# Two output terms summed ahead of the matmul, and low parts of weights by a negating copy and an accumulating transfer, in the state-space stage of a decoder kernel

## The chip, the cores and the metric

The kernel runs on one core of a Trainium2 chip. The metric is device microseconds of one execution; the profile gives its own span, from the first to the last instruction, beside it.

## What is computed

The reference is a trunk of two layers for 512 tokens of width 1024, in float32. Layer 0 mixes tokens by gated delta-net and sliding-window heads, layer 1 by an S5 state-space mixer. After the mixer each layer has cross-attention into 256 memory tokens and a SwiGLU feed-forward part; every sub-layer ends in a residual sum and a layer norm. The change lies in the S5 mixer of layer 1:

```python
def s5_mixer(u, a_re, a_im, log_dt, b_re, b_im, c_re, c_im, d_skip, w_o, w_g):
    ...
    bu = jnp.einsum('gph,bsgh->bsgp', b_bar, ug.astype(jnp.complex64))
    _, states = lax.associative_scan(_lin_rec_combine, (a_seq, bu), axis=1)
    y = (jnp.einsum('ghp,bsgp->bsgh', c_re.astype(f32), states.real)
         - jnp.einsum('ghp,bsgp->bsgh', c_im.astype(f32), states.imag))
    y = y.reshape(bsz, s, d) + d_skip.astype(f32) * uf
    hid = jax.nn.gelu(y).astype(u.dtype)
    return (hid @ w_o) * jax.nn.sigmoid(hid @ w_g)
```

## The kernel before

**Matmuls in three parts.** A float32 product is made of float32r products. Each operand is kept as a high part (`hi`, rounded to float32r) and a low part (`lo`, what the rounding left out), and `mm3` issues three matmuls: high by high, high by low, low by high. Weights come from DRAM a piece of 512 KB at a time (`_load`): SyncE issues the transfer into `raw` (2 buffers), ScalarE copies it to `hi` (4 buffers), and VectorE subtracts `hi` from `raw` into `lo` (4 buffers). `weights` calls `_load` with a priority of 200 places ahead of the program (`AHEAD`).

**The order.** No instruction is issued while the program is written down. The class `Order` records each call with its operands, and `issue` then simulates the engines by the costs in `cost` and by a single DMA channel, and gives each engine the first instruction in program order whose operands and buffers are there. What comes out is a fixed queue for each engine. The name of a line in the profile is therefore always the same (L422, in `issue`), and groups are told apart by their tiles: `ps` is a PSUM bank, `big` a tile of 128x2048, `t` a temporary of 128x512 (13 buffers), `tiny` one of 128x64.

**The S5 stage.** `s5` goes through 8 blocks of 4 pairs of groups (128 channels each). For each block it loads two table tiles of 1 MB from the scratch in DRAM (`s5m`), transposes the tokens, makes `br` and `bi` (the input products) with 8 float32 matmuls, turns them back with six VectorE operations into `x` and `y`, scans both along the chunks, and turns them forward again: `r1`, `r2`, `i1`, `i2`, each a product of a scan result and a table, shifted by one chunk, with a small memset on GpSimd for the first column. The output bank `yp` is then summed on TensorE for each of 4 pairs from four products: the taps inside the chunk, `r1` and `r2` with table 4, and `i1 - i2` with table 5. GELU, four transposes and a split into high and low part follow.

**Fill.** Between the blocks `s5` takes steps of other work: after each block one step of `fill`, which is the key projection of the second layer (`mem_k(1)`, 4 column blocks with 2 weight loads each), then the value projection (`mem_v(1)`, 2 halves with 4 loads each); from block 5 on also the first half of the gate (`glu_gate`, 4 loads). The value projection holds its 4 loads until both token tiles are done. Just ahead of the stage stands the layer norm of layer 0's feed-forward part, whose result the first transposes read.

Of the kernel before, what the change touches and what calls it, by code (L numbers as in the profile page):

```python
# [92 lines left out]
class Engine:  # L93
    """Records the calls of an engine instead of issuing them."""
# [10 lines left out]
class Order:  # L105
    """The order in which the recorded instructions are issued: for each engine, the first in program
    order of those whose operands are there, by estimates of what the instructions take."""
# [12 lines left out]
    def either(self, *calls):  # L120
        """The same result by one of several engines: (engine, function, args, kwargs)"""
        self.add(list(calls))
# [7 lines left out]
    # ---- what an access touches  # L130
# [40 lines left out]
    @staticmethod  # L171
    def operands(fn, args, kw):
        isap = lambda x: hasattr(x, "ap") and hasattr(x, "tensor")
        conv = lambda x: x if isap(x) else (x[:] if hasattr(x, "mls") else None)
        outs, ins = [], []
        for n, x in [("out" if k == 0 else "", x) for k, x in enumerate(args)] + list(kw.items()):
            x = conv(x)
            if x is None:
                continue
            (outs if n in ("out", "accum_out") else ins).append(x)  # L180
        if fn == "tensor_tensor_reduce":
            outs.append(ins.pop())
        if fn == "matmul" and not kw["start"]:
            ins.append(outs[0])
        return outs, ins

    def cost(self, eng, fn, outs, ins, kw):
        o = outs[0]
        n = 1
        for _, c in list(o.ap)[1:]:  # L190
            n *= c
        psum = any("PSUM" in str(x.space) for x in ins)
        if eng == "pe":
            if fn == "transpose":
                return 0.11
            r = ins[0].dtype == F32R
            if r:
                return (n if n >= 256 else max(4 * n, 128)) / 2400.0 + 0.0035
            m = list(ins[0].ap)[-1][1]
            return (4 * n if n >= m else 2 * (n + m)) / 2400.0 + 0.004  # L200
        if eng == "act":
            ptr = sum(1 for k in ("bias", "scale") if hasattr(kw.get(k), "tensor")) + ("accum_out" in kw)
            return n / 1200.0 + (0.05 if psum else 0.095) + 0.093 * ptr
        if eng == "dve":
            fast = fn in ("tensor_copy", "tensor_scalar", "memset") and not psum and "PSUM" not in str(o.space)
            if fn == "reciprocal":
                return 0.0063 * n + 0.07
            if fn in ("tensor_reduce", "bn_stats"):
                n = max(n, max(_size(x) for x in ins))
            ptr = 0.06 if any(_size(x) == 1 for x in ins) else 0.0  # L210
            return (n / 1.92 if fast else n / 0.96) / 1000.0 + 0.07 + ptr
        if eng == "pool":
            if kw.get("op") == OP.pow:
                return 0.165 * n + 0.3
            return n * 0.00085 + 0.03 if fn == "memset" else n * 0.0022 + 0.1
        return 0.45

    # ---- recording
# [50 lines left out]
    # ---- ordering  # L269
    def order(self, seq, prio):  # L270
# [44 lines left out]
        while len(out) < n:  # L315
# [5 lines left out]
            for e in self.eng:  # L321
# [53 lines left out]
                if e == "sp":  # L375
                    busy[e] = now + a[4]
                    nbytes = max(_bytes(x) for x in op.outs + op.ins)
                    s = max(now + 1.65, dma_free)
                    dma_free = s + nbytes / 3.6e5
                    op.done = dma_free + 0.75  # L380
                else:
                    cost = a[4]
                    if e == "pe":
                        if now - busy[e] > 3.4:
                            slow = now + 3.4
                        cost += min(cost, max(slow - now, 0.0) * 0.5)
                    busy[e] = now + cost
                    op.done = busy[e]
# [55 lines left out]
class Trunk:  # L444
    def __init__(self, tc, a, stack, dbg=None):
        self.tc, self.nc, self.a, self.dbg = tc, tc.nc, a, dbg or {}
        self.o = Order(tc)
        self.n = 0
        self.stack = stack
        pool = lambda name, bufs, **k: stack.enter_context(tc.tile_pool(name=name, bufs=bufs, **k))  # L450
        self.cp = pool("const", 1)
        self.bigp = pool("big", 16)
        self.wp = pool("w", 2)
        self.tp = pool("t", 2)
        self.ps = pool("ps", 8, space=bass.MemoryType.PSUM)
        self.dram = pool("dram", 1, space=bass.MemoryType.DRAM)
# [20 lines left out]
    def weights(self, w, k0, n, c0, width):  # L477
        """n row tiles of w by `width` columns as high and low parts, fetched ahead of the program"""
# [8 lines left out]
    def _load(self, view, n, w, steps=1, between=None):  # L487
# [4 lines left out]
        for s in range(steps):  # L492
# [5 lines left out]
            self.o.V.tensor_tensor(lo[:, cs], raw[:, cs], hi[:, cs].bitcast(F32), op=OP.subtract)  # L498
# [8 lines left out]
    def gemm_feat(self, w, c0, cols, act, n, sink, early=0):  # L507
        """out[feature, token], 256 columns of w at a time; act(kt) -> (hi, lo) of [128, n]. The first
        `early` column blocks take the first half of the tokens before the second."""
# [39 lines left out]
    def gemm_tok_steps(self, w, k0, nk, c0, act, ntt, sink, tail=0):  # L549
        """out[token, 512 columns of w at c0]; act(kt, tt) -> (hi, lo) of [128, 128]. The last `tail`  # L550
        steps of the contraction go one token tile after the other."""
# [20 lines left out]
    def transposes(self, src, n, width=P):  # L572
        """n blocks of [128, width] from src to one bank [width, n, 128]"""
# [9 lines left out]
    def mixer0(self, fill):  # L583
# [6 lines left out]
        # ---- x, transposed  # L590
# [14 lines left out]
        # ---- constants  # L605
# [19 lines left out]
        # ---- rotary tables  # L625
# [14 lines left out]
        # ---- beta and decay logits, feature-major then token-major  # L640
# [57 lines left out]
        # ---- delta-net q, k, v  # L698
# [44 lines left out]
        # ---- the decay inside a chunk, [j, (head, i)]  # L743
# [24 lines left out]
        # ---- chunk matrices, [j, (head, i)]: L^T above its diagonal  # L768
# [25 lines left out]
        # ---- q and v  # L794
# [3 lines left out]
        # ---- inverse of the 32 x 32 diagonal blocks, one system a partition (h, c, b)  # L798
# [17 lines left out]
        # ---- the products of q and k under the decay  # L816
# [12 lines left out]
        # ---- the gate of the delta-net heads  # L829
# [8 lines left out]
        # ---- merge the blocks: X' = X - X E X for 32, 64  # L838
# [41 lines left out]
        # ---- sequential part over chunks  # L880
# [80 lines left out]
        # ---- the sliding-window heads  # L961
# [57 lines left out]
    def feat_view(self, bigs):  # L1019
        """tiles of 2 feature tiles each -> at(kt) of [128, (hi, lo), 512], act(kt), act(kt, tt)"""  # L1020
# [9 lines left out]
    def residual_sinks(self, half, alpha, eps, g, b, last, after):  # L1030
        """z = alpha h + sublayer in place of h; on the last half the norm, then after(tt, h)"""
# [41 lines left out]
    def to_feat(self, vs):  # L1073
        """after-norm step: the token tile transposed into the feature-major operand"""
        return lambda tt, n, x: self.block_to_feat(vs, n, slice(tt * P, (tt + 1) * P), x)
# [147 lines left out]
    # ---- S5  # L1223
    def s5_params(self):
        """per state (g2, p) on partitions and pair of groups q: the discretised coefficients"""
# [20 lines left out]
        # exp(lam) - 1 = 2 t / (1 - t), t = tanh(lam / 2)  # L1246
# [27 lines left out]
        # (a_bar - 1) / a, with a_bar - 1 = (e - 1) - 2 e sin^2(theta / 2) + i e sin(theta)  # L1274
# [17 lines left out]
    def s5_tables(self):  # L1292
        """the matrices of a chunk of 4 tokens for each pair of groups, left in DRAM by blocks of 4 pairs"""
# [5 lines left out]
        # rotations by 0..15 chunks, and by 0, 16, .., 112  # L1299
# [57 lines left out]
        # B [(g2, p), q, h] and C [(g2, p), q, h]  # L1357
# [5 lines left out]
        # the skip on the diagonal of the first tap  # L1363
# [3 lines left out]
        for b in range(8):  # L1367
# [11 lines left out]
            # rotation tables  # L1379
# [12 lines left out]
            # chunk input and output matrices  # L1392
# [28 lines left out]
            # decay over a chunk, none into the first  # L1421
# [4 lines left out]
            # taps inside a chunk  # L1426
# [26 lines left out]
    def s5(self, fill):  # L1453
        """the mixer's output in feature-major form; with it the gate of the first half of the columns"""
# [3 lines left out]
        for b in range(8):  # L1458
# [15 lines left out]
            # turned back by the rotation of each chunk: x - i y  # L1474
# [12 lines left out]
            # forward again, one chunk later; the real part's products meet in the output's sum  # L1487
# [6 lines left out]
            r1, r2, i1, i2 = turned(x, cs), turned(y, sn), turned(x, sn), turned(y, cs)  # L1494
            V.tensor_tensor(i1, i1, i2, op=OP.subtract)
            terms = ((r1, 4), (r2, 4), (i1, 5))
            yp = self.bank()
            for q in range(4):
# [3 lines left out]
                for n, (z, m) in enumerate(terms):  # L1502
                    T.matmul(yo, q1(z, q), kc(m), start=False, stop=n == 2)
# [49 lines left out]
    def exp(self, out, x, w):  # L1553
        """exp to float32: 2^n by the exponent's bits, a polynomial on what is left"""
# [14 lines left out]
    def reduced(self, ang, tmp):  # L1569
        """an angle of any size less a multiple of 2 pi, in parts"""  # L1570
# [18 lines left out]
    def build(self):  # L1589
# [13 lines left out]
        for _ in range(PRE):  # L1603
            next(kv)
        gtok = self.s5(kv)
        self.glu(gtok)
# [28 lines left out]
def layouts(v):  # L1635
    """the inputs as the kernel reads them: small operands with the index that goes on partitions first"""
# [31 lines left out]
```

## Time and profile before

| | us |
|---|---|
| runs | 1576.44, 1580.3, 1572.28 |
| median of the runs | 1576.44 |
| span of the profiled execution | 1572.0 |
| TensorE busy / VectorE busy / ScalarE busy / GpSimd busy | 1539.2 / 990.3 / 550.9 / 58.2 |

The profile gives one execution; its time beside the span is not listed by itself, the nearest of the runs is 1572.28. Busy times are sums over the span. TensorE's records overlap and their ends are modelled, so its busy time is not a measure of the rate at which it works; the distance from one start to the next is.

### The profile page before, as it was taken

How to read it: one execution, taken by the hardware profiler on the slowest of the kernel's cores; microseconds unless marked ns; L12 is line 12 of the kernel's file. 1: busy time of each engine (PE TensorE's matmuls, PEld its weight loads, DVE VectorE, ACT ScalarE, POOL GpSimd, SP SyncE). 2: the span in 40 equal slices, each digit the busy share in tenths (PEclk: the TensorE clock that was granted, in tenths of full speed). 3: DMA queues.
4: the chain of work that ended last, by engine and by line, in shares of the span. 5: the costliest groups of instructions: out<-in, count | busy, mean ns of one | idle time of the engine just before them, and what ended most of it. 6: DMA issues, size and time to landing. Idle time of an engine off the chain costs nothing.

```text
span 1572.0 us, 20938 instructions
## 1 busy us (share of the span) xinstructions
PE 1539.2 (98%) x8132; PEld 1300.8 (83%) x8132; DVE 990.3 (63%) x1890; ACT 550.9 (35%) x988; POOL 58.2 (4%) x97
## 2 busy tenths in 40 slices
PE   7999999999999999999999899999999999999998
PEld 5887878778988888888888798888888888888886
DVE  6989666556557788725754899748657443334436
ACT  6533436424432344423441233332422322222211
POOL 1100000000000000010000000000000000000000
PEclk9999999999999999999999999999999999999999
DMA  6423224125314344526572554323213333233322
GB/s 184 125 60 95 81 89 134 51 71 168 91 37 132 111 166 163 183 84 201 188 254 81 201 176 148 125 94 108 88 37 98 107 102 100 73 115 96 105 68 94
DMA packets 125539, 184.06 MB, mean 117 GB/s; under 512 B 14144, under 2 KB 84800, under 8 KB 121344
## 3 DMA queue, kind: packets, MB, share of 16 engines
q1 hardware_dynamic: 125440, 182.73, 36.0%
q8 instruction: 64, 1.05, 0.3%
q14 instruction: 35, 0.29, 0.1%
HBM read 162.52 MB, written 20.19 MB: 116 GB/s over the span
## 4 chain that ended last, share of the span: by engine, by line
PE 83%; DVE 10%; DMA 2%; ACT 2%; issue 1%; SPq 0%; POOL 0%; DVEq 0%; ACTq 0%; POOLq 0%
PE ps L422 83%; DVE t L422 5%; DVE big L422 3%; DVE lo L422 2%; ACT big L422 1%; ACT hi L422 1%; DVE tiny L422 1%; DMA raw<-in_xv_w_dram 1%; DMA t<-in_x_t_dram 1%; DMA raw<-in_xo_w_dram 0%; DMA raw<-in_hyb_w_in_dram 0%; ACT L422 0%; DMA raw<-in_hyb_w_out_dram 0%; ACT t L422 0%; DMA prm<-in_dn_a_log_dram 0%
## 5 line engine op out<-in xcount | busy, mean ns | idle before, releaser
L422 PE MATMUL ps<-big,hi 128*128 128x512 f32 (+1 forms) x2368 | 651.4, 361 | 6.4 <-ACT hi L422 4.9
L422 PE MATMUL ps<-hi,big 128*128 128x512 f32 x1728 | 548.1, 395 | 1.1 <-DVE big L422 0.7
L422 PEld LDWEIGHTS ps<-big,hi 128*128 128x128 f32 x2368 | 422.1, 191 | 70.0 <-ACT hi L422 5.3
L422 DVE TENSOR_TENSOR lo<-raw,hi 128x1024 fp32r<-128x1024 f32 (+2 forms) x252 | 303.5, 1205 | 222.8 <-ACT hi L422 220.1
L422 ACT ACTIVATE hi<-raw 128x1024 fp32r<-128x1024 f32 (+2 forms) x252 | 263.5, 1046 | 512.2 <-PE ps L422 356.4
L422 PE MATMUL ps<-big,lo 128*128 128x512 f32 (+1 forms) x1184 | 426.7, 362 | 2.7 <-DVE lo L422 2.6
L422 PEld LDWEIGHTS ps<-hi,big 128*128 128x128 f32 x1728 | 323.2, 188 | 66.5 <-DVE big L422 1.6
L422 PE MATMUL ps<-lo,big 128*128 128x512 f32 x864 | 339.1, 394 | 4.6 <-DVE lo L422 4.5
L422 PEld LDWEIGHTS ps<-big,lo 128*128 128x128 f32 x1184 | 225.5, 191 | 34.8 <-DVE lo L422 3.8
L422 PEld LDWEIGHTS ps<-lo,big 128*128 128x128 f32 x864 | 162.8, 188 | 40.3 <-DVE lo L422 8.0
L422 ACT ACTIVATE big<-ps 128x256 fp32r<-128x256 f32 (+2 forms) x196 | 93.9, 514 | 223.2 <-PE ps L422 214.2
L422 DVE TENSOR_TENSOR big<-ps,big 128x256 fp32r<-128x256 f32 (+1 forms) x160 | 82.2, 545 | 63.0 <-ACT big L422 61.1
L422 ACT ACTIVATE t<-ps 128x512 f32<-128x512 f32 (+4 forms) x129 | 64.5, 510 | 161.9 <-PE ps L422 157.9
L422 DVE SCALAR_TENSOR_TENSOR big<-big,ps 128x512 f32<-128x512 f32 x56 | 38.3, 685 | 95.4 <-PE ps L422 95.4
L422 DVE SCALAR_TENSOR_TENSOR t<-t,ps 128x512 f32<-128x512 f32 x72 | 48.9, 681 | 58.5 <-ACT t L422 53.5
L422 PE MATMUL ps<-big,big 128*128 128x256 f32 (+6 forms) x392 | 72.3, 340 | 0.1
L422 ACT ACTIVATE big<-t 32x128 f32<-32x128 f32 (+1 forms) x140 | 59.9, 443 | 30.6 <-DVE t L422 13.2
L422 PEld LDWEIGHTS ps<-big,t 128*128 128x128 f32 (+2 forms) x496 | 59.4, 186 | 10.8 <-issue 3.6
L422 PE MATMUL ps<-big,t 128*128 128x128 f32 (+3 forms) x496 | 65.5, 276 | 1.8 <-DVE t L422 1.7
L422 DVE SCALAR_TENSOR_TENSOR big<-big,tiny,t 128x512 f32<-128x512 f32 x96 | 66.6, 744 | 0.0
L422 PE MATMUL ps<-ident,t 128*128 128x128 f32 x336 | 60.2, 274 | 3.7 <-ACT t L422 1.9
L422 PEld LDWEIGHTS ps<-big,big 128*128 128x128 f32 (+1 forms) x392 | 54.2, 189 | 8.6 <-issue 1.9
(140 smaller groups left out, 927.7 us busy)
## 6 DMA issues: line engine op xcount, KB each, us to landing
raw<-in_ffn_wg_dram SPq DMA_DIRECT2D x44, 512.0 KB, 3.5
raw<-in_ffn_wu_dram SPq DMA_DIRECT2D x44, 512.0 KB, 3.5
raw<-in_ffn_wd_dram SPq DMA_DIRECT2D x44, 512.0 KB, 3.9
s5m<-big SPq DMA_DIRECT2D x16, 1024.0 KB, 4.4
big<-s5m SPq DMA_DIRECT2D x16, 1024.0 KB, 5.2
raw<-in_hyb_w_in_dram SPq DMA_DIRECT2D x26, 512.0 KB, 3.9
raw<-in_xk_w_dram SPq DMA_DIRECT2D x16, 512.0 KB, 4.9
raw<-in_xv_w_dram SPq DMA_DIRECT2D x16, 512.0 KB, 3.8
```

What stands on the lines that cost most here:

```text
L422: op.inst = getattr(self.eng[e], fn)(*args, **kw)
```

## The change

In `s5`, `r1` and `r2` are added on VectorE, in place, and the sum goes through one product with table 4 in place of two. During `s5` (that is, for the loads recorded there: the keys and values of the second layer and the first half of the gate) `_load` makes the low part in another way: ScalarE writes the negated copy of `raw` to `lo`, rounded as `hi` is, and a transfer issued from GpSimd reads the weights from DRAM once more and adds them to `lo`. The subtraction on VectorE goes. The order's model gets a cost of 1.2 us for a DMA issue on GpSimd, treats it as a DMA of the same channel as SyncE's, and counts an accumulating transfer's destination as an input. Comments and docstrings are dropped throughout, which is left out here.

```diff
@@ operands @@
-        if fn == "matmul" and not kw["start"]:
+        if fn == "matmul" and not kw["start"] or kw.get("accum_op"):
             ins.append(outs[0])
@@ cost @@
         if eng == "pool":
+            if fn == "dma_start":
+                return 1.2
@@ order @@
-                if e == "sp":
+                if a[1] == "dma_start":
                     busy[e] = now + a[4]
                     nbytes = max(_bytes(x) for x in op.outs + op.ins)
                     s = max(now + 1.65, dma_free)
@@ _load @@
             self.o.A.activation(hi[:, cs], raw[:, cs], AF.Copy)
-            self.o.V.tensor_tensor(lo[:, cs], raw[:, cs], hi[:, cs].bitcast(F32), op=OP.subtract)
+            if self.low_by_dma:
+                self.o.A.activation(lo[:, cs], raw[:, cs], AF.Copy, scale=-1.0)
+                self.o.G.dma_start(r(lo)[:, ks], view[:, ks], accum_op=OP.add)
+            else:
+                self.o.V.tensor_tensor(lo[:, cs], raw[:, cs], hi[:, cs].bitcast(F32), op=OP.subtract)
@@ s5 @@
             r1, r2, i1, i2 = turned(x, cs), turned(y, sn), turned(x, sn), turned(y, cs)
+            V.tensor_tensor(r1, r1, r2, op=OP.add)
             V.tensor_tensor(i1, i1, i2, op=OP.subtract)
-            terms = ((r1, 4), (r2, 4), (i1, 5))
+            terms = ((r1, 4), (i1, 5))
...
-                    T.matmul(yo, q1(z, q), kc(m), start=False, stop=n == 2)
+                    T.matmul(yo, q1(z, q), kc(m), start=False, stop=n == 1)
@@ build @@
+        self.low_by_dma = True
         gtok = self.s5(kv)
+        self.low_by_dma = False
```

The lines that the model of a DMA goes on with are the same in both kernels:

```python
                    dma_free = s + nbytes / 3.6e5
                    op.done = dma_free + 0.75
```

## Rows read from the trace of the kernel before

**Rows 1.** The page: its span, and the chain that ended last by engine

```profile
span 1572.0 us, 20938 instructions
...
PE 83%; DVE 10%; DMA 2%; ACT 2%; issue 1%; SPq 0%; POOL 0%; DVEq 0%; ACTq 0%; POOLq 0%
```

**Rows 2.** Busy time by 15 us stretches of 885 to 1005 us

```profile
core 0: us, PE busy (x) PEld busy (x) DVE busy (x) ACT busy (x) POOL busy (x), PEclk, DMA share, GB/s
...
900.00:915.00 15.00, 12.94 (x85) 12.73 (x86) 12.68 (x18) 4.18 (x7) 0.32 (x3) 0.77 0.52 176
...
960.00:975.00 15.00, 14.36 (x90) 12.05 (x89) 15.00 (x22) 4.10 (x7) 0.42 (x4) 1.00 0.13 41
...
sum 120.00, PE 113.48 PEld 103.24 DVE 111.05 ACT 41.20 POOL 4.16; mean PE 14.19 PEld 12.90 DVE 13.88 ACT 5.15 POOL 0.52
```

**Rows 3.** The chain inside 875 to 1010 us: start, us, what

```profile
879.68 1.07 ACT hi L422
...
882.60 1.14 DVE lo L422
...
894.54 4.78 DVE t L422 x8
...
902.75 9.10 PE ps L422 x53
```

**Rows 4.** Busy time by longer and shorter stretches, columns as in rows 2

```profile
870.00:930.00 60.00, 55.21 (x387) 52.06 (x386) 54.04 (x84) 16.46 (x23) 4.42 (x17) 0.94 0.58 211
930.00:1005.00 75.00, 73.27 (x457) 63.84 (x457) 69.93 (x99) 26.86 (x41) 1.70 (x16) 1.00 0.37 122
...
885.00:890.00 5.00, 4.47 (x38) 4.27 (x36) 4.96 (x12) 0.00 (x0) 1.51 (x6) 1.00 1.03 413
```

**Rows 5.** Groups by shape, 885 to 1005 us: count, busy us, mean ns, idle before

```profile
L422 PE MATMUL ps<-big,t 128*128 128x128 f32 x226 | 30.1, 279 | 1.2 <-DVE t L422 1.1
...
L422 PE MATMUL ps<-t,big 128*128 128x128 f32 x128 | 16.4, 275 | 0.0
...
L422 ACT ACTIVATE hi<-raw 128x1024 fp32r<-128x1024 f32 x20 | 21.1, 1058 | 20.7 <-DMA raw<-in_xk_w_dram 10.1 <-PE ps L422 8.5 <-DMA raw<-in_xv_w_dram 1.2
```

**Rows 6.** TensorE in order of time: start, us, operation, idle before

```profile
883.56 0.40 PE L422 MATMUL ps<-big,hi 128*128 128x256 f32 x2
...
890.77 1.97 PE L422 MATMUL ps<-ident,big 128*128 128x128 f32 x16 [1.30 <-DVE big L422]
...
902.75 0.58 PE L422 MATMUL ps<-big,lo 128*128 128x256 f32 x1 [2.06 <-DVE lo L422]
...
951.61 3.06 PE L422 MATMUL ps<-big,t 128*128 128x128 f32 x26
954.43 0.48 PE L422 MATMUL ps<-lo,big 128*128 128x512 f32 x1
```

**Rows 7.** VectorE in order of time, columns as in rows 6

```profile
896.26 0.68 DVE L422 TENSOR_TENSOR t<-t,t 128x512 f32<-128x512 f32 x1
896.86 0.68 DVE L422 TENSOR_TENSOR t<-ps,big 128x512 f32<-128x512 f32 x1
```

**Rows 8.** The page's DMA issues: count, KB each, median us to landing

```profile
raw<-in_xk_w_dram SPq DMA_DIRECT2D x16, 512.0 KB, 4.9
raw<-in_xv_w_dram SPq DMA_DIRECT2D x16, 512.0 KB, 3.8
...
raw<-in_s_glu_wg_dram SPq DMA_DIRECT2D x8, 512.0 KB, 4.7
```

**Rows 9.** Issues into the raw tiles, 862 to 1000 us: ns min/median/max

```profile
L422 SPq DMA_DIRECT2D raw<-in_xk_w_dram x8: 367/368/389, 862.8 to 909.5; - x8
```

**Rows 10.** DMA issues from 870 to 930 us, columns as in rows 8

```profile
big<-s5m SPq DMA_DIRECT2D x8, 1024.0 KB, 8.4
```

**Rows 11.** The transfers of the tables, 800 to 1000 us

```profile
DMA to landing us min/median/max: 5.2/5.2/11.7
```

More of the change, by code (lines that the diff above doesn't have):

```diff
@@ L1604, in build @@
             next(kv)
+        self.low_by_dma = True
         gtok = self.s5(kv)
+        self.low_by_dma = False
         self.glu(gtok)
```

## The prediction

> **What bounds the kernel now.** I read the page first. TensorE holds 83% of the chain that ended last [rows 1], which says little yet: its records overlap, so a TensorE that looks busy can still lose time between matmuls. So I went to the stage that the change touches. The S5 stage runs from about 885 to 1005 us: the state-space blocks, filled up with the second layer's key and value projections and the first half of the gate. In its 15 us stretches [rows 2] the reader is to see that VectorE is as full as TensorE: 111.05 us of 120 against 113.48, and 15 of 15 in the middle, where TensorE has 14.36. The chain inside the stage [rows 3] changes sides: a subtraction that makes a low part (`lo`), runs of VectorE pieces on the temporaries, then a run of 53 matmuls. So neither engine alone sets the stage; each is a few per cent from being the bound. Two more things matter. Around 885 us the DMA engines are full (share 1.03, 413 GB/s) [rows 4]. And TensorE's granted clock, 2.4 GHz elsewhere in the stage, is 0.77 in the mean from 900 to 915 us, so part of that stretch went at 1.2 GHz [rows 2], after TensorE had waited several times.
>
> **Matmuls removed: -7.0 us.** Each of 8 blocks drops one of the four products for each of 4 pairs: 32 matmuls. An f32 matmul of this shape stands in the trace as two records: the 64 products that make `br` and `bi` are 128 records [rows 5]. So 64 records go. What one costs TensorE is the distance between starts, not its 279 ns: 26 of them start at 951.61 and the next instruction at 954.43 [rows 6], 2.82/26 = 0.1085 us. 64 x 0.1085 = 6.9, taken as 7.0. The bound on the other side is busy time over count, 30.1/226 = 0.133 [rows 5], or 8.5. This counts only where TensorE is the bound.
>
> **One add a block on VectorE: nothing.** A 128x512 add of two temporaries holds it 0.60 us (896.26 to 896.86 [rows 7]); 8 x 0.60 = 4.8 us. What hides it is the time freed by the 20 subtractions (of the loads in [rows 8], which are for both layers and both halves: 8 for keys, 8 for values, 4 for the gate), each 1.14 us in the chain [rows 3], 22.8 us; net VectorE loses 18 us of work in a stage where it is full. Without that cover the add would cost the 4.8.
>
> **VectorE freed: -3.1 us.** It can only give back time in which TensorE waits. TensorE idles 120 - 113.48 = 6.5 us in the stage [rows 2]. Of that 1.30 stands before the first transposes, which wait for the layer norm, and 2.06 at 902.75 for a low part [rows 6], whose raw weights had come late: ScalarE waited 10.1 us for the keys' weights [rows 5]. Neither ends with VectorE's load. 6.5 - 1.3 - 2.1 = 3.1. The bounds are 0 (other short waits take their place) and 6.5, which adds what the lower clock costs, 15 x 0.23 = 3.4 us [rows 2]. I leave the clock as it is, since the part on the first low parts puts a gap near the same place.
>
> **Negating copies on ScalarE: nothing.** 20 copies like the one of 1.06 us that makes `hi` [rows 5] are 21 us; ScalarE is busy for 41.20 of 120 us [rows 2], so its gaps hold them. Without that cover a PSUM eviction queued behind one comes up to 1.06 us late.
>
> **Issues on GpSimd: nothing.** The kernel before issues no DMA from GpSimd. The price of an issue there is bounded below by SyncE's 0.37 us [rows 9]; above I take the 1.2 us that the new line in the order's costs sets. 20 x 1.2 = 24 us on an engine with 4.16 us of work in the stage [rows 2]. Queued behind an issue that waits for its copy are the small memsets of the turned tiles, four a block; the new add reads their column, so VectorE can wait for them: 1.2 us in each of 8 blocks, 9.6 us, which the 18 us freed cover.
>
> **The first low parts: +4.8 us.** Today `hi` of the first key weights starts at 879.68 on ScalarE [rows 3], and the 48 matmuls of the first key block fill TensorE from 883.56 until 1.30 us before the transposes at 890.77 [rows 6], 5.9 us in which the layer norm runs and TensorE has nothing else. After: copy done at 880.75, negation at 881.8, issue, landing. The shortest landing of a weight load is 3.8 us [rows 8]; the 1 MB table loads of this very stretch, in which the DMA engines are full, take 8.4 in the median [rows 10] and 11.7 at most [rows 11]. So `lo` comes between 885.6 and 893.5, and up to 0.8 us (1.2 - 0.37) later by the issue. I take 890, since the stretch is full. The third matmul of the group needs it, so all 5.9 us of key matmuls move behind the norm and lengthen a stage that is then TensorE's. Against that, the norm loses the subtraction at 882.60, which stands in its chain [rows 3]: S5 starts 1.1 us earlier. 5.9 - 1.1 = 4.8. Bounds: `lo` at 885.6 lets TensorE wait 1.8 us after its first two matmuls, +0.7; `lo` at 894.3 with the transposes queued behind the waiting matmul adds 3.5, +8.3.
>
> **The later low parts: +6.0 us.** 20 loads go through 4 `lo` buffers: five passes, the first priced above. In each, a new low part can start only when TensorE lets go of a buffer. Today the subtraction follows the copy at once. The order written for the changed kernel allows by its own formulas about 0.95 us for the negating copy and 1.65 + 1.46 + 0.75 us for a DMA with free engines, 4.8 in all, and puts other matmuls there. TensorE's queue is fixed, so what comes later than that stalls it. By the rows: 1.06 + 4.9 (median landing of the key weights [rows 8]) + 0.4 (half of 0.8, the issue) = 6.4, so 1.6 a pass; I take 1.5, 4 passes. Bounds: landing 3.8 gives 4.9, nearly 0 a pass; landing 8.4 with 0.8 for the issue gives 10.3, 5.5 a pass, 22 us.
>
> The Trainium skill, "DMA: Bandwidth & Descriptors", section "Anatomy of one DMA — SWDGE (gpsimd) path", fits a transfer issued from GpSimd by 2.0 us plus its bytes over 436 GB/s; for 512 KB that is an estimate of 3.2 us, shorter than any landing in [rows 8], and by it the later passes would cost nothing and the sum would be 6 us lower. The Trainium skill, "Collectives: The Full Stack", section "The bandwidth ceiling: the fold count and why AG ≠ RS ≠ AR", says that an adding transfer reads two sources where a copy reads one, and so runs at about half its rate; this speaks against the change, and the trace of before, which has no adding transfer, can't show it.
>
> **Sum.** -7.0 - 3.1 + 4.8 + 6.0 = +0.7 us on a span of 1572.0 [rows 1]. Little lies around that span: the nearest run is 1572.28. The median of the runs is 1576.44, 4.4 above the span, so I forecast 1577 us. The three runs spread over 8 us; 0.5% (7.9 us) is about what a measurement can tell from no change.
>
> **Rival 1: the order hides every low part.** Landings stay at 3.8 us or below, and TensorE has S5 work meanwhile. Then -7.0 - 3.1 + 0.7 + 0 = -9.4, or 1567; with the clock never falling another -3.4, 1564. For it: VectorE has 18 us less to do, so S5 matmuls are ready earlier. Against: the first landing falls in the full stretch. The fit in the Trainium skill's "DMA: Bandwidth & Descriptors" is on its side.
>
> **Rival 2: the adding transfers become the bound (slower).** From 870 to 1005 us DMA is busy for 0.58 x 60 + 0.37 x 75 = 62.6 us and moves 21.8 MB [rows 4], 350 GB/s while busy, so a 512 KB load takes 1.5 us of all engines. If each addition takes twice that, 20 of them take 60 us, and 122 of 135 us are gone, the first half of the stage wholly. Each later pass is then some 4 us late and the first costs its upper bound: -7.0 - 3.1 + 8.3 + 16 = +14, or 1591. It decides once a later pass costs over (7.9 + 5.3)/4 = 3.3 us beyond the plan, that is from a landing of some 6.6 us. For it: the key loads already wait for DMA. Against: from 930 us on the share is only 0.37. The rule on two reads in the Trainium skill's "Collectives: The Full Stack" would bring it about.
>
> **Rival 3: VectorE freed gives nothing, the low parts cost little.** -7.0 + 4.8 + 1 = -1.2, 1575: hardly to be told from the forecast, and counted with it.
>
> **How the numbers follow.** Forecast with rival 3: 0.45; rival 1: 0.25, of which a little ends within 0.5%; rival 2: 0.30. So faster by over 0.5% 0.24, within 0.5% 0.46, slower 0.30. The extremes of the terms are -8.5 - 6.5 + 0.7 + 0 = -14 and -7.0 + 8.3 + 22 = +23, so 1562 and 1600. Cutting about a tenth at each end leaves 1564 to 1595.
>
> **What the changed profile would show.** The group of products on temporaries 64 records shorter; VectorE clearly less busy than TensorE from 915 to 990 us; 20 transfers of 512 KB issued from GpSimd, and their landing, the number on which most hangs; TensorE idle from about 884 to 890 us and the key matmuls behind the first transposes; TensorE's later waits ended by a DMA into `lo`. The prediction is wrong if those waits sum to under 3 us or over 16, or if the clock stays down for much longer than now.

## The result, and the profile after

The changed kernel takes 1592.95 us in the median of 4 runs (1591.27 to 1596.88); the kernel before, run beside it, 1574.88. The ratio is 1.0103, 95% interval 1.0065 to 1.0141: slower. The profiled execution is the one of 1591.27, span 1589.5. (Here and below a median is over all runs of a kernel, and the ratios leave out the executions in the chip's slower state.)

The page of the changed kernel, the parts that answer to [rows 1] and [rows 8], with the DMA queues (packets, MB, share of 16 engines' span):

```profile
span 1589.5 us, 20852 instructions
...
q1 hardware_dynamic: 125440, 182.73, 36.4%
q0 software_dynamic: 7488, 10.49, 3.9%
...
PE 82%; DMA 6%; DVE 6%; ACT 2%; issue 2%; SPq 0%; POOL 0%; DVEq 0%; ACTq 0%; POOLq 0%
...
big<-s5m SPq DMA_DIRECT2D x16, 1024.0 KB, 8.6
...
raw<-in_xk_w_dram SPq DMA_DIRECT2D x16, 512.0 KB, 8.3
```

DMA has taken VectorE's place in the chain (6%, from 2%; VectorE 6%, from 10%). The new queue's 20 transfers take 3.9% of 1589.5 us, 62 us of all 16 engines, 3.1 us each. And the loads beside them suffer: key weights land after 8.3 us in the median where [rows 8] has 4.9.

Busy time by 15 us stretches, to be held against [rows 2] and [rows 4] (the last columns are the granted clock, the DMA share, GB/s):

```profile
885.00:900.00 15.00, 6.64 (x46) 6.64 (x47) 4.70 (x10) 2.97 (x4) 1.15 (x5) 0.66 1.10 304
900.00:915.00 15.00, 11.41 (x97) 10.95 (x96) 15.00 (x25) 4.73 (x7) 3.10 (x7) 1.00 1.01 273
...
930.00:945.00 15.00, 13.23 (x88) 13.01 (x87) 9.66 (x16) 5.03 (x7) 1.89 (x4) 0.77 0.91 223
945.00:960.00 15.00, 13.03 (x93) 12.39 (x92) 11.47 (x19) 8.53 (x12) 4.68 (x8) 0.89 0.95 246
960.00:975.00 15.00, 14.78 (x91) 12.80 (x90) 12.14 (x19) 7.67 (x11) 2.65 (x6) 1.00 0.99 246
...
sum 150.00, PE 124.34 PEld 111.13 DVE 101.99 ACT 59.77 POOL 25.46; mean PE 12.43 PEld 11.11 DVE 10.20 ACT 5.98 POOL 2.55
```

The table runs to 1035 us, since the stage is longer. VectorE is still full from 900 to 915 us, behind the late start, but has room after it (12.14 of 15 from 960 to 975 us, where it had 15.00). TensorE has not gained by it: it idles 150 - 124.34 = 25.7 us. The DMA engines, at a share of 0.13 between 960 and 975 us before, are at 0.99.

What TensorE waited for from 862 to 1040 us (us in total, times, longest), and the low parts' transfers in the same stretch:

```profile
PE ps L424 <- DMA lo<-in_xk_w_dram: 14.7, 3, 9.6
PE ps L424 <- DMA lo<-in_xv_w_dram: 5.8, 3, 3.6
PE ps L424 <- DVE t L424: 4.5, 3, 1.9
...
PE ps L424 <- DMA lo<-in_s_glu_wg_dram: 0.7, 1, 0.7
```

```profile
L424 POOL DMA_DIRECT2D lo<-in_xk_w_dram x8: 1282/1284/1461, 880.6 to 934.9; - x8
L424 POOL DMA_DIRECT2D lo<-in_xv_w_dram x8: 1188/1194/1199, 944.6 to 998.1; - x8
...
DMA to landing us min/median/max: 7.8/9.9/16.4
```

The first wait in TensorE's order of time, then VectorE's end of the layer norm and its next work:

```profile
883.32 0.40 PE L424 MATMUL ps<-big,hi 128*128 128x256 f32 x2
893.36 0.58 PE L424 MATMUL ps<-big,lo 128*128 128x256 f32 x1 [9.65 <-DMA lo<-in_xk_w_dram]
893.74 0.63 PE L424 MATMUL ps<-big,hi 128*128 128x256 f32 x2
...
896.09 1.73 PE L424 MATMUL ps<-ident,big 128*128 128x128 f32 x13
...
902.37 0.40 PE L424 MATMUL ps<-big,hi 128*128 128x256 f32 x2
```

```profile
885.79 2.73 DVE L424 SCALAR_TENSOR_TENSOR big<-big,tiny,t 128x512 f32<-128x512 f32 x4
898.75 2.48 DVE L424 TENSOR_TENSOR t<-ps,big 128x512 f32<-128x512 f32 x4 [10.23 <-PE ps L424]
```

Two key matmuls run, the third waits for its low part until 893.36, and the transposes, which started at 890.77 in [rows 6], stand behind it in the fixed queue and start at 896.09. VectorE had ended the norm, which the transposes read, at 888.52, so they stood 7.6 us behind a matmul that they don't need. After the wait a pair of matmuls is written as 0.63 us where a few us later it is 0.40: TensorE works at 1.2 GHz for a while, and the stretch's granted clock is 0.66.

**The account.** The 64 records gone are worth -7.0. TensorE waits 14.7 + 5.8 + 0.7 = 21.2 us for transfers into `lo` (0.7 of it for the gate). From its first key matmul on it idles 25.7 us in the table and the 1.3 us of the first wait that lie ahead of 885 us, 27.0; less the 21.2 that is 5.8, against 6.5 before [rows 2], -0.7. The lowered clock costs, as an estimate, the busy time of a stretch times what is missing of the clock: 6.64 x 0.34 + 13.23 x 0.23 + 13.03 x 0.11 = 6.7 us, against 12.94 x 0.23 = 3.0 before [rows 2], +3.7. -7.0 + 21.2 - 0.7 + 3.7 = +17.2, and the spans differ by 17.5.

### The profile page after: what moved, and what is told of

The parts are those of the page before. It is cut to its first block, busy times and chain, and to the rows that moved or that the text cites. A ratio compares the mean times of both kernels' runs of the same rounds, so it can differ in the third digit from the quotient of the medians.

```text
span 1589.5 us, 20852 instructions
## 1 busy us (share of the span) xinstructions
PE 1536.2 (97%) x8068; PEld 1297.2 (82%) x8068; DVE 973.5 (61%) x1878; ACT 568.3 (36%) x1008; POOL 83.0 (5%) x117
## 4 chain that ended last, share of the span: by engine, by line
PE 82%; DMA 6%; DVE 6%; ACT 2%; issue 2%; SPq 0%; POOL 0%; DVEq 0%; ACTq 0%; POOLq 0%
PE ps L424 82%; DVE t L424 2%; DVE big L424 2%; DMA lo<-in_xk_w_dram 2%; DVE lo L424 1%; DMA lo<-in_xv_w_dram 1%; DMA raw<-in_xv_w_dram 1%; ACT big L424 1%; DMA raw<-in_s_glu_wg_dram 1%; DMA t<-in_x_t_dram 1%; ACT hi L424 1%; DVE tiny L424 1%; DMA raw<-in_s_glu_wo_dram 0%; DMA raw<-in_hyb_w_in_dram 0%; ACT lo L424 0%
## 5 line engine op out<-in xcount | busy, mean ns | idle before, releaser
L424 PE MATMUL ps<-big,lo 128*128 128x512 f32 (+1 forms) x1184 | 427.5, 362 | 15.4 <-DMA lo<-in_xk_w_dram 14.7
L424 DVE TENSOR_TENSOR lo<-raw,hi 128x1024 fp32r<-128x1024 f32 (+2 forms) x232 | 279.3, 1205 | 223.2 <-ACT hi L424 220.9
L424 POOL TENSOR_TENSOR tiny<-tiny,mhalf 128x1 f32<-128x1 f32 (+1 forms) x28 | 25.1, 896 | 960.7 <-DVE tiny L424 952.0
L424 PE MATMUL ps<-big,t 128*128 128x128 f32 (+3 forms) x432 | 57.5, 276 | 3.7 <-DVE t L424 3.5
```

Of the source, the lines that this page charges most:

```text
L424: op.inst = getattr(self.eng[e], fn)(*args, **kw)
```

## The experiments

All medians in us; the ratio is to the kernel before on the same chip. Only e3 and e11 keep the changed kernel's order of instructions on every engine. In the others `issue` plans the order anew for the edited program, so a difference of a few us can also come from another order.

| run | what differs from the changed kernel | median | ratio, 95% interval |
|---|---|---|---|
| e1 | low parts by VectorE | 1578.47 | 1.0017, 0.9997 to 1.0037 |
| e2 | three products | 1602.95 | 1.0173, 1.0124 to 1.0222 |
| e3 | transfers copy, don't add | 1574.23 | 0.9993, 0.9962 to 1.0025 |
| e4 | order knows of double bytes | 1600.88 | 1.0163, 1.0118 to 1.0209 |
| e5 | keys' low parts by VectorE | 1578.75 | 1.0026, 1.0001 to 1.0051 |
| e6 | one block's tables for all | 1585.37 | 1.0070, 1.0048 to 1.0092 |
| e7 | e6 with low parts by VectorE | 1576.66 | 1.0022, 0.9997 to 1.0048 |
| e8 | low parts by GpSimd | 1599.21 | 1.0146, 1.0103 to 1.0190 |
| e9 | no transfer at all | 1560.82 | 0.9936, 0.9906 to 0.9966 |
| e10 | first two loads by VectorE | 1593.98 | 1.0154, 1.0110 to 1.0198 |
| e11 | half the columns added | 1581.58 | 1.0055, 1.0039 to 1.0072 |
| e12 | e9 with three products | 1568.76 | 0.9965, 0.9951 to 0.9978 |

**The sum alone (e1).**

```diff
-        self.low_by_dma = True
+        self.low_by_dma = False
```

> The two terms are summed ahead of the matmul; the low parts are made by VectorE as before, with no transfer from GpSimd. Theory A (the adding transfers cost all of the loss): the loss is gone; of the 7.0 us of matmuls removed, up to 4.8 us go to the adds on a VectorE that is full in this stage, so 1568 to 1576 us beside some 1575 of the kernel before. Rival B (the extra add lengthens the VectorE chain and is itself a part of the loss): 1578 to 1583.

1578.47, over theory A's range and just inside rival B's; the ratio's interval reaches the kernel before, so at best nothing is gained from 64 records less. VectorE has the adds on top of its subtractions. Its load beside TensorE's, then TensorE's waits for its temporaries from 862 to 1040 us, in e1 and in the kernel before:

```profile
900.00:1005.00 105.00, 95.03 (x586) 83.59 (x587) 96.99 (x139) 34.02 (x51) 2.35 (x24) 0.93 0.41 134
```

```profile
PE ps L424 <- DVE t L424: 5.8, 8, 2.1
```

```profile
PE ps L422 <- DVE t L422: 2.4, 5, 0.8
```

96.99 of 105 us for VectorE, and TensorE at 95.03 with the clock at 0.93. With the low parts and the other tiles TensorE waits 11.3 us for VectorE, where it waited 6.4 before. So rival B has this much right: the add is no gift while VectorE makes the low parts. But most of the changed kernel's loss is not here: with the transfers it is 1592.95 in place of 1578.47.

**The transfers alone (e2).**

```diff
@@ rope_sink, layer 0 @@
-                V.tensor_tensor(r1, r1, r2, op=OP.add)
-                tp = self.transposes(lambda k: r1[:, k * P:(k + 1) * P], 4)
+                    tp = self.transposes(lambda k: r1[:, k * P:(k + 1) * P], 4)
@@ s5 @@
-            V.tensor_tensor(r1, r1, r2, op=OP.add)
-            terms = ((r1, 4), (i1, 5))
+            terms = ((r1, 4), (r2, 4), (i1, 5))
```

> The low parts by copy and adding transfer, but the three products as before, 64 records more on TensorE. Theory A: TensorE stalls on transfers most of the stage, so the 7 us of matmuls are partly hidden in the stalls: 1593 to 1599 us, against 1593 of the changed kernel. Rival B (the sum is what cost): 1578 to 1585.

1602.95, over the upper end of theory A by 4 and 10.0 over the changed kernel. Not all of that is the 64 records. By an oversight this kernel also differs in layer 0, far ahead of the stage: the add of the rotary embedding is left out, and its transposes, moved into the loop above them, are made twice, 32 records more on TensorE. Its first key matmul, to be held against 883.32:

```profile
888.94 0.40 PE L424 MATMUL ps<-big,hi 128*128 128x256 f32 x2
```

So 5.6 us of the 13.0 between the two spans lie ahead of the stage, and 7.4 from there to the end. Chance has a part in the 5.6 too: e9 and e3 start at 886.4 and 886.7 without that edit. With the transfers the 64 records are worth some 7 us, and theory A's guess that they would partly vanish in the stalls was wrong.

**Copies in place of additions (e3), and half the columns added (e11).** Both have the changed kernel's order on every engine; for that e11 also counts the bytes of a transfer from GpSimd twice in the order's model, so that half a transfer stands there as a whole one.

```diff
-                self.o.G.dma_start(r(lo)[:, ks], view[:, ks], accum_op=OP.add)
+                self.o.G.dma_start(r(lo)[:, ks], view[:, ks])                                      # e3
+                self.o.G.dma_start(r(lo)[:, ks, :w // 2], view[:, ks, :w // 2], accum_op=OP.add)   # e11
@@ order, e11 alone @@
-                    nbytes = max(_bytes(x) for x in op.outs + op.ins)
+                    nbytes = max(_bytes(x) for x in op.outs + op.ins) * (2 if e == "pool" else 1)
```

> The same queues on all engines as the changed kernel, but the transfers from GpSimd copy the weights into the low parts and don't add (the low parts are wrong). Theory A (an addition takes the 16 engines twice as long as a copy, and the DMA engines are full): the software queue's share falls from 3.9% of the span to about 2%, the landing into lo from 9.9 us in the median to 5 to 7, and the time by 8 to 14 us, to 1579 to 1585. Rival C (the way through GpSimd itself, its issue and its place in the queues, costs the time whatever the transfer does): within 4 us of the changed kernel, 1589 to 1594.

> The same queues on all engines as the changed kernel, but each adding transfer covers the first half of the columns only (the low parts of the other half are wrong), 256 KB in place of 512. Theory A (it is the time that additions take of the 16 engines): the software queue's share falls to about 2%, the landing to 5 to 7 us, and the time to 1573 to 1581, near that of whole copies that don't add. Rival G (an adding transfer has a long latency of its own, whatever its size): landing 8 us or more, 1586 to 1593.

e3 took 1574.23, the whole loss gone and 5 us more than expected; e11 1581.58, just over theory A's range. First e3's queue, landing and all of TensorE's waits for low parts, then the same of e11:

```profile
q0 software_dynamic: 7488, 10.49, 2.4%
...
L424 POOL DMA_DIRECT2D lo<-in_xk_w_dram x8: 742/742/910, 883.9 to 934.8; - x8
...
DMA to landing us min/median/max: 4.3/6.2/13.1
...
PE ps L424 <- DMA lo<-in_xk_w_dram: 7.7, 1, 7.7
```

```profile
q0 software_dynamic: 7488, 5.24, 2.3%
...
L424 POOL DMA_DIRECT2D lo<-in_xk_w_dram x8: 1282/1284/1461, 881.4 to 933.9; - x8
...
DMA to landing us min/median/max: 5.4/7.5/13.5
...
PE ps L424 <- DMA lo<-in_xk_w_dram: 11.6, 3, 8.1
PE ps L424 <- DMA lo<-in_xv_w_dram: 4.4, 3, 2.1
```

A copy of 512 KB takes 2.4% of 1576.8 us over 20, 1.9 us of all engines; an addition 3.1, 1.6 times as much. And with copies TensorE waits for a low part once, the first time; every later wait is gone. Halving the bytes brings the additions to the engine time of copies and gives back 11.4 of the 18.7 us that separate e3 from the changed kernel. The other 7.4 stay with the same engine time: the issue on GpSimd takes 1.28 us for an addition of either size and 0.74 for a copy, and the landing is 7.5 against 6.2, between what theory A and rival G had for it. Rival C (the way through GpSimd, whatever the transfer does) falls as the cause of the loss, and so does rival G (size doesn't matter); how the 7.4 divide between the issue and the addition's own latency is left open.

**An order that knows (e4).**

```diff
-                    nbytes = max(_bytes(x) for x in op.outs + op.ins)
+                    nbytes = max(_bytes(x) for x in op.outs + op.ins) * (2 if e == "pool" else 1)
```

> The changed kernel, but the order counts an adding transfer's bytes twice, so that it knows of 1.46 us more for each and of the longer queue. Rival D (the plan is too hopeful, and TensorE's fixed queue stalls for that): the first wait of 9.65 us goes, as S5 work stands ahead of it, and the time falls by 8 us or more, to 1585 or below. Theory A (the transfers' capacity is used up): the work is put in another order but the DMA engines stay over 0.9 full, 1587 to 1594.

1600.88, 8 us more than the changed kernel. The first wait is still there, 9.53 us:

```profile
903.02 0.58 PE L424 MATMUL ps<-big,lo 128*128 128x256 f32 x1 [9.53 <-DMA lo<-in_xk_w_dram]
917.79 0.77 PE L424 MATMUL ps<-big,t 128*128 128x128 f32 x2 [5.04 <-DVE t L424]
```

So rival D falls as I put it: counting the bytes twice doesn't mend the order. Theory A's range was missed as well, by 7 us; the new order has a wait of 5.04 us for VectorE, but that the order itself is what costs was not shown.

**Which loads (e5, e10).**

```diff
-            if self.low_by_dma:
+            if self.low_by_dma and "xk" not in view.tensor.name:                                   # e5
+            if self.low_by_dma and not ("xk" in view.tensor.name and self.first_keys > 0):         # e10, 2 loads
```

> The changed kernel, but the low parts of the 8 key loads are made by VectorE; the 12 of values and gate stay with copy and adding transfer. Theory A1 (most of the loss lies in the first stretch, where the table loads fill the DMA engines): 10 us or more come back, 1577 to 1583. Rival F (the loss is spread evenly over the 20 loads): 8/20 of 18 us come back, 1584 to 1588.

> The changed kernel, but the first two key loads, which feed the block that waited 9.65 us, have their low parts made by VectorE; 18 adding transfers stay. Theory A1 (the first wait and the clock that falls behind it are most of the loss): 9 us or more come back, 1578 to 1584. Rival J (the full DMA engines only put the wait elsewhere): 1586 to 1593.

e5 came to 1578.75, in theory A1's range: 14.2 of 18 us back for 8 loads of 20. e10 gave back nothing: 1593.98, 1 us over rival J's range. (Its profiled execution, 1610.64, is the longest of its runs; it lost time to a low clock in layer 0, so its times stand some 18 us late.) Its waits, then those of e5:

```profile
PE ps L424 <- DMA lo<-in_xv_w_dram: 10.7, 2, 7.0
PE ps L424 <- DMA lo<-in_xk_w_dram: 10.2, 2, 5.9
```

```profile
PE ps L424 <- DMA lo<-in_xv_w_dram: 3.7, 2, 2.7
PE ps L424 <- DVE lo L424: 3.2, 1, 3.2
```

With the first pair exempt the 9.65 us wait is gone and 20.9 us of waits for low parts stand later, as much as the 21.2 of the changed kernel: rival J. With all eight key loads exempt TensorE waits 6.4 us (3.7 and 2.7 for the gate). So the cost isn't the first wait by itself; it is the key additions together, in the first half of the stage, where the table loads run too.

**Room on the DMA engines (e6, and e7 as its control).**

```diff
-            blks = [self.big(F32) for _ in range(2)]
-            self.o.SP.dma_start(blks[0], self.s5m[b][:, :2048])
-            self.o.SP.dma_start(blks[1], self.s5m[b][:, 2048:])
+            if b == 0:
+                blks = [self.big(F32) for _ in range(2)]
+                self.o.SP.dma_start(blks[0], self.s5m[b][:, :2048])
+                self.o.SP.dma_start(blks[1], self.s5m[b][:, 2048:])
```

> The changed kernel, but all 8 blocks use the tables of the first (a wrong output), so that 14 of the 16 table loads, 14 MB and by the rows some 40 us of all DMA engines, are gone; the 20 adding transfers stay. Theory A (capacity): the landing into lo falls from 9.9 us in the median to about 6, and the kernel comes within 5 us of its control with VectorE's low parts, the next run. Rival G (an adding transfer takes long by itself, whatever else flows): landing still 8 us or more, and 10 us or more above the control.

> The control: all 8 blocks use the tables of the first (a wrong output), terms summed, low parts by VectorE. Theory A: table loads hold nothing up here but the first blocks, 1570 to 1578. Rival G says the same; if it falls below 1568, the table loads were a bound of their own already.

1585.37 and 1576.66: the transfers cost 8.7 us here where they cost 14.5 beside the table loads (1592.95 - 1578.47). That lies between what the two theories gave for the time; for the landing rival G was right. e6 from 900 to 930 us, and its landing:

```profile
900.00:930.00 30.00, 29.36 (x252) 28.98 (x251) 27.30 (x45) 18.14 (x27) 8.12 (x13) 1.00 0.97 198
```

```profile
DMA to landing us min/median/max: 6.4/8.5/10.3
```

Without the tables the longest landing falls from 16.4 to 10.3 us and the median only from 9.9 to 8.5, and 0.97 of the engines is still in use for 198 GB/s: the additions for the keys, with their loads, come close to filling them alone. So part of the cost is the company of the table loads, and the larger part is the additions' own.

**Low parts on GpSimd (e8).**

```diff
-                self.o.A.activation(lo[:, cs], raw[:, cs], AF.Copy, scale=-1.0)
-                self.o.G.dma_start(r(lo)[:, ks], view[:, ks], accum_op=OP.add)
+                self.o.G.tensor_tensor(lo[:, cs], raw[:, cs], hi[:, cs].bitcast(F32), op=OP.subtract)
```

> Terms summed, and the 20 low parts subtracted on GpSimd, which has little to do in the stage: no copy on ScalarE, no transfer. Theory A (the idea of freeing VectorE is right, the transfers are what costs): VectorE loses its 20 subtractions, TensorE is the bound, 1563 to 1571. Rival H (GpSimd takes much longer than VectorE for a subtraction, or the two hinder each other): its subtractions take over 3 us, VectorE's operations in the stage get longer, 1575 to 1590.

1599.21: rival H, by its second half, and 9 us over its range. GpSimd takes 2.4 us in the median, not over 3, but VectorE's operations get longer, and TensorE waits 28.4 us for VectorE (862 to 1040 us). e8, then two of the groups in the changed kernel:

```profile
L424 DVE TENSOR_TENSOR_SCAN t<-big,t 128x512 f32<-128x512 f32 x12 | 25.7, 2153 | 0.0
L424 DVE TENSOR_TENSOR t<-t,big 128x508 f32<-128x508 f32 x24 | 23.3, 1008 | 0.0
...
L424 DVE TENSOR_TENSOR t<-ps,big 128x512 f32<-128x512 f32 x24 | 15.5, 680 | 4.4 <-PE ps L424 4.4
```

```profile
L424 DVE TENSOR_TENSOR_SCAN t<-big,t 128x512 f32<-128x512 f32 x13 | 15.4, 1214 | 0.0
L424 DVE TENSOR_TENSOR t<-t,big 128x508 f32<-128x508 f32 x24 | 15.0, 680 | 0.0
```

The scan takes 2153 ns here in the mean and 1214 in the changed kernel, the product of two SBUF tiles 1008 and 680, the product with a PSUM bank 680 and 684. The Trainium skill, "SBUF — State Buffer", section "Who interferes with whom", says that a VectorE instruction with two SBUF inputs contends with a GpSimd instruction that reads SBUF, and that one with at most one SBUF input, outside the 2-port modes, doesn't. These rows agree.

**The ceiling, and the square (e9, e12).** The transfer is left out; the low parts stay the negated copies.

```diff
-                self.o.G.dma_start(r(lo)[:, ks], view[:, ks], accum_op=OP.add)
```

> The ceiling of the idea: terms summed, low parts only the negated copy of ScalarE, with no transfer and no subtraction (the low parts are wrong). Prediction's step (freeing VectorE and TensorE is worth about 10 us when the low parts cost nothing): 1561 to 1568. Rival I (another wait takes the place, and the idea gives little even with free low parts): 1570 to 1576.

> As the run without transfers (low parts only the negated copy, so they are wrong), but with the three products as before the change. It completes the square of the two edits: sum alone, free low parts alone, both. Theory K (VectorE is the bound of the stage before; freed of its 20 subtractions it leaves TensorE as the bound, and only then the 64 records count): 1566 to 1570, that is some 6 us below the kernel before, and 6 to 8 above the run with both. Rival L (the two edits add up by themselves): as the sum alone gave nothing or lost 3 us, this run would be at 1558 to 1561.

e9: 1560.82, e12: 1568.76, both as the first theory of each had it (e9 a fraction below its range). e9 by stretches:

```profile
930.00:1005.00 75.00, 74.14 (x435) 63.04 (x434) 64.67 (x98) 35.05 (x48) 1.68 (x16) 1.00 0.41 137
```

TensorE 74.14 of 75 us at full clock, VectorE 64.67: the stage is TensorE's. The square of the two edits:

| | low parts by VectorE | low parts free (e9, e12) | low parts by transfers |
|---|---|---|---|
| three products | 1574.5 (before) | 1568.76 | 1602.95 (e2, part of it from layer 0) |
| two products | 1578.47 (e1) | 1560.82 | 1592.95 (changed) |

The sum loses up to 4 us where VectorE makes the low parts and gains 8 where they are free. Free low parts and the sum together are worth 13 us by the medians, 10 by the ratio, and the transfers cost 32. Of these 32 the addition is 18.7, by e3; the other 13.4 (1574.23 - 1560.82) come with plain copies already, though e9 has an order of its own. So a second read of the weights from GpSimd would have eaten the whole gain without any addition. None of the versions that compute the reference beat the kernel before; e1 and e5 come nearest.

## Why the prediction came out as it did

The forecast was 1577 and "within 0.5%"; the time is 1592.95, inside the range and slower. What happened is rival 2, put at 1591 with a chance of 0.30: the range held because it was drawn to take rival 2 in, and the mechanism of the forecast itself was the wrong one. One of its own signs says so: the clock stays down for longer than before, in three stretches of 15 us where it had been one. The other sign, later waits for low parts of over 16 us, is met only with the first wait counted in: 21.2 with it, 11.6 without.

- **Both engines near the bound: right.** The square shows it: the sum alone gives nothing, free low parts alone 5 to 6 us, both together 13.
- **Matmuls removed, -7.0, "only where TensorE is the bound": the size right.** 8 us between e12 and e9, some 7 between e2 and the changed kernel, nothing in e1. In the changed kernel TensorE stands still for 27 us, and they count even there.
- **The add hidden by the subtractions removed: right.** With the subtractions gone the sum gains its 8 us (e12 to e9). Without that cover e1 has it: the 7 us are gone and up to 4 more, where I had 4.8 for the add.
- **VectorE freed, -3.1: somewhat low.** Free low parts with three products give 5 to 6 us (e12), within the bound of 6.5. With both edits 13 by the medians, 10 by the ratio, against the 10.1 of the two terms.
- **Copies on ScalarE and memsets on GpSimd at nothing: nothing speaks against it.** e9 has the same 20 negating copies and is the shortest of all. Among TensorE's waits ScalarE stands with 1.0 us; no wait of VectorE for a memset stands among those listed. The issue is 1.19 to 1.46 us, at and over the upper bound of 1.2.
- **The first low parts, +4.8: mis-sized, and the place of the wait was wrong.** I had `lo` at 890 and the key matmuls moved behind the norm. It came at 893.36, near the upper end, and the transposes were queued behind the wait, so they started 5.3 us later, with most of the key matmuls still to do: the case of the upper bound, 8.3. The norm did end earlier, by 2.9 us (888.52, from 891.38) where I had 1.1, but nothing could use it. And e10, whose order is another, shows that taking this wait away gains nothing, since as much comes up later.
- **The later low parts, +6.0: the step that failed.** I priced the landing with 4.9 us, the median of weight loads from SyncE, plus 0.4. It was 9.9 in the median, 7.8 at least. With 9.9 in the same formula (the landing is counted from the issue, so the 0.4 is in it), 1.06 + 9.9 - 4.8 = 6.2 a pass, 25 us for four passes, it would have been over the 22 of the bound. The waits after the first measured 21.2 - 9.65 = 11.6; that other matmuls cover the rest was not shown. That it is the landing that decides, e3 shows with the same order: at 6.2 us in the median, under the 6.6 that rival 2 gave as its limit, no later wait is left and the time is 1574.23.
- **The clock: left out.** I kept it as before; by the estimate of the account it cost 6.7 us where it had cost 3.0.

Why the landing was so long: rival 2 had the DMA engines at 122 of 135 us. Measured from 885 to 1005 us, the changed kernel, then e3:

```profile
885.00:1005.00 120.00, 97.86 (x639) 88.99 (x639) 79.89 (x126) 50.01 (x69) 24.26 (x47) 0.91 0.96 238
```

```profile
885.00:1005.00 120.00, 106.83 (x708) 97.11 (x707) 90.21 (x141) 56.54 (x77) 17.68 (x50) 0.94 0.80 259
```

0.96 of 120 us with 238 GB/s, and copies with more bytes at 0.80. The Trainium skill, "Collectives: The Full Stack", section "The bandwidth ceiling: the fold count and why AG ≠ RS ≠ AR", says of collectives that ReduceScatter has half of AllGather's rate because its add needs two source reads. Carried over to this transfer it points the right way: 1.6 times the engine time in e3's comparison, about twice the 1.5 us that I had worked out for a load from SyncE. That it is the second read was not shown. The fit in the Trainium skill's "DMA: Bandwidth & Descriptors", section "Anatomy of one DMA — SWDGE (gpsimd) path", gives an estimate of 3.2 us. That is under even the shortest copy from GpSimd here, 4.3 us, with other traffic beside it.

## What to carry to other kernels

Before moving work from a full engine to the DMA engines, work out their share in that very stage with the new transfers at their own price: here it came to 0.96, and nothing was free. Price an adding transfer at 1.6 times a copy issued the same way, as it measured here, and its landing not by quiet loads but by what lands in that stretch. Where two engines are both near the bound, an edit that shifts work from one to the other shows nothing alone; leave the suspected cost out altogether (e9) to see what the idea could give before building on how it is paid for. And with a fixed order one late operand holds up all that is queued behind it, and here the granted clock fell to 0.66 in that stretch; taking away the first such wait (e10) only showed the next.

## What the runs showed of the hardware that was not expected

An addition issued from GpSimd holds it 1.28 us for 1 KB rows and 1.19 for 2 KB rows, the same with half the bytes in as many rows; a copy 0.74 and 0.70. A GpSimd subtraction of 128x1024 takes 2.4 us and stretches VectorE's scans beside it from 1.21 to 2.15 us in the mean.
